# The first loads of a decoder trunk: host layout by partition, another order and other queues

## The chip, the cores and the metric

The kernel runs on one core of a Trainium2 chip. The metric is the device time in microseconds of one execution. Before, three runs took 1038.72, 1039.44 and 1039.55 us, so the median is 1039.44.

## The reference

A trunk of four layers works on 512 tokens of width 1024 in float32: latent attention (MLA), an MLP, gated linear attention (GLA), an MLP. Each is preceded by a root-mean-square norm and added to the residual x. Only the start of the first layer bears on this change:

```python
def rms_norm(x, gain):
    xf = x.astype(jnp.float32)
    y = xf * lax.rsqrt(jnp.mean(xf * xf, axis=-1, keepdims=True) + EPS)
    return (y * gain.astype(jnp.float32)).astype(x.dtype)

def mla_mixer(xn, positions, w_in, q_norm, w_uq, kv_norm, w_ukv, w_o):
    h = xn @ w_in
    c_q = h[..., :Q_LORA]
    c_kv = h[..., Q_LORA:Q_LORA + KV_LORA]
    k_rope = h[..., Q_LORA + KV_LORA:]
    q = (rms_norm(c_q, q_norm) @ w_uq).reshape(B, S, MLA_HEADS, QK_NOPE + QK_ROPE)
    kv = (rms_norm(c_kv, kv_norm) @ w_ukv).reshape(B, S, MLA_HEADS, QK_NOPE + V_HEAD)
```

`w_in` has 1024 rows and 704 columns: 384 for the query, 256 for key and value, 64 for the rotary key. Other weights that the text speaks of: an MLP's up weights have 4096 columns, the GLA's input weights 3088.

## The kernel before

x is kept transposed: `xT` has eight chunks of 128 features (partitions) by 512 tokens. The first projection is therefore a sum over eight chunks k. Products are made in three parts: every operand is split into an upper part (rounded to float32r, written by ScalarE with a Copy) and a lower part (the rest, written by VectorE), and TensorE adds upper x upper, lower x upper and upper x lower. `split` (L122) makes the two parts of weights, `scaled` (L272) the two parts of an x chunk times its norm weight; the token's own norm factor is applied later, which is why the matmuls can start before any sum of squares is known.

The opening is written at the end of `trunk_kernel`. The raw weights of key and value, `raw0` (`wraw_ckv`), come in five pieces (`load_part`, L1683: chunks 0, 1, 2 to 3, 4 to 5, 6 to 7), x in eight (`load_x`, L186), the norm weights with positions in one small load (`gains`, L1689). ScalarE issues x chunks 0 and 1 on its own queue, SP all else. Meanwhile TensorE works on nine matmuls on a tile of ones (L1701). Then for each piece the weights are split (L1704) and the x chunks of that piece scaled (L1707); `tc.keep_in_program_order` holds these ScalarE instructions in the written order. Everything else is placed by a scheduler that orders each engine's instructions by its own estimates, so an edit can move instructions that it does not name.

`mla` (L401) then multiplies. L436 is the projection to key and value, six matmuls for each chunk into two banks, 48 in all. L132 to L134 (`mm3`) are the query's three column blocks: two from `raw` of L444, in two halves of four chunks, and the last from `col_chunk` at L459, loaded at L154. That last load takes the buffer of `wraw_ckv`, so it waits until the last of its splits has read it. `latent` (L410) reads a finished bank twice on ScalarE (L411, L413) and on VectorE (L414, L416). `nrm.square` (L455) forms the squares of x on ScalarE (L265) and sums them on VectorE (L266). The rotary columns are loaded at L467. The means of the three norms are matmuls: L482 of x, L484 of key and value, L486 of the query.

Loads from SP and ScalarE share eight semaphores in turn, so each load waits until the one eight before it has landed.

The rows of `w_in` are 2,816 bytes long. A piece of the key and value weights is thus read in runs of 1 KB, the last query columns in runs of 512 B, the rotary ones in 256 B. An x chunk is 128 runs of 2 KB that lie end to end.

Of the kernel before, what the change touches and what calls it, by code (L numbers as in the profile page):

```python
# [18 lines left out]
P = 128  # L19
# [3 lines left out]
ND = D // P  # L23
# [5 lines left out]
ROPE = 64  # L29
# [21 lines left out]
def trunk_kernel(ctx: ExitStack, tc: tile.TileContext, t_in: dict, out: bass.AP):  # L51
# [70 lines left out]
    def split(src, hi, lo, hi_eng=ACT, lo_eng=DVE, order=lambda i: i):  # L122
        if hi_eng is ACT:
            order(ACT.activation(hi, src, AF.Copy))  # L124
        else:
            hi_eng.tensor_copy(hi, src)
        lo_eng.tensor_tensor(lo, src, f(hi), ALU.subtract)  # L127
# [35 lines left out]

    def piece(raw, a, n, order=lambda i: i, at=(W_AT, W_AT)):
        hi = room_for("wh", a, n, at[0])
        lo = room_for("wl", a, n, at[1])
        split(raw, hi, lo, order=order)
        return hi, lo
# [14 lines left out]
    xT = [xall[:, j] for j in range(ND)]  # L183
    x_in = t_in["x"].rearrange("(j p) t -> p j t", p=P)

    def load_x(q, j):  # L186
        q.dma_start(xall[:, j], x_in[:, j])

# [212 lines left out]
    def mla(layer, nrm, first, pools):  # L401
        w_in = t_in["mla_w_in"][layer]
        w_uq = t_in["mla_w_uq"][layer].rearrange("(k p) (h c) -> p k h c", p=P, h=MH)
# [38 lines left out]
        for h in range(2):  # L442
            ks = slice(h * KH, (h + 1) * KH)
            SP.dma_start(raw[:, ks], w_in[:, :256].rearrange("(k p) n -> p k n", p=P)[:, ks])  # L444
            wq.append(piece(raw[:, ks], KH, 256))
# [12 lines left out]

        raw = col_chunk(w_in, 256, P)  # L459
        w = piece(raw, ND, P)  # L460
# [5 lines left out]

        raw = col_chunk(w_in, QL + KL, ROPE)  # L467
        wr = room_for("wh", ND, 2 * ROPE).rearrange("p k (a b) -> p k a b", a=2)
# [1211 lines left out]
    raw0 = sb.tile([P, ND, 256], F32, tag="wraw", bufs=2, name="wraw_ckv")  # L1680
    src0 = t_in["mla_w_in"][0][:, QL : QL + KL].rearrange("(k p) n -> p k n", p=P)

    def load_part(k0, k1):  # L1683
        SP.dma_start(raw0[:, k0:k1], src0[:, k0:k1])

    load_x(ACT, 0)
    load_part(0, 1)
    load_x(ACT, 1)
    SP.dma_start(gains, t_in["gains"])  # L1689
    load_part(1, 2)  # L1690
    load_part(2, 4)
    load_x(SP, 2)
    load_x(SP, 3)
    for k in (4, 6):
        load_part(k, k + 2)
        load_x(SP, k)
        load_x(SP, k + 1)
    exp_set()
# [4 lines left out]
    for k0, k1 in ((0, 1), (1, 2), (2, 4), (4, 6), (6, 8)):  # L1703
        w = piece(raw0[:, k0:k1], k1 - k0, KL, tc.keep_in_program_order)  # L1704
        w0 += [(w, i) for i in range(k1 - k0)]
        for j in range(k0, k1):
            nrm.scaled(j, xT[j], tc.keep_in_program_order)  # L1707
# [41 lines left out]
_INS = [  # L1749
    "mla_w_in", "mla_w_uq", "mla_w_ukv", "mla_w_o", "gla_w_in", "gla_w_gk_up", "gla_w_o",  # L1750
    "mlp_w_up", "mlp_w_down",
# [21 lines left out]


def layout(inputs):
    arrs = {n: np.ascontiguousarray(inputs[n]) for n in _INS}
    arrs["x"] = np.ascontiguousarray(np.asarray(inputs["x"])[0].T)
    gains = np.concatenate([np.asarray(inputs[n]).reshape(-1, P) for n in GAINS]).T
    positions = np.ascontiguousarray(np.asarray(inputs["positions"]).reshape(NT, P).T)
    inv_freq = np.array([[float.fromhex(v) for v in _INV_FREQ]] * P, dtype=np.float32)  # L1780
    arrs["gains"] = np.ascontiguousarray(np.concatenate([gains, positions.view(np.float32), inv_freq], axis=1))
    arrs["fin_row"] = np.ascontiguousarray(np.asarray(inputs["final_norm"]).reshape(1, D))
    return arrs
# [11 lines left out]
```

## Time and profile before

| what | before |
|---|---|
| median of three runs | 1039.44 us |
| the profiled execution, its own time | 1039.75 us |
| its span | 1038.0 us |
| granted TensorE clock | 0.999 |
| TensorE matmuls busy | 1028.6 us, 99% |
| VectorE busy | 879.2 us, 85% |
| ScalarE busy | 694.5 us, 67% |
| first matmul of the projection (L436) | 5.55 us after the span's start |
| first matmul of the query projection (L132) | 17.63 us |

Times in the profile count from the start of the span. PE is TensorE (PEld its weight loads), DVE VectorE, ACT ScalarE, POOL GpSimd; SPq and ACTq are the queues on which SP and ScalarE issue DMAs. A row of the view in order of time gives the start, the busy time, the engine and line, the tile written and the tile read, and how often; in brackets stand the idle time ahead and what ended it. A DMA row's last number is the time from issue to landing.

### The profile page before, as it was taken

What the parts mean: (1) busy time and instruction counts of PE and PEld (TensorE: products, weight loads), DVE (VectorE), ACT (ScalarE), POOL (GpSimd) and SP (SyncE); (2) the same over time, 40 slices, a digit from 0 to 9 for tenths busy, and PEclk for the clock granted to TensorE, in tenths of its full rate; (3) what the DMA queues carried; (4) which work ended last, traced back from release to release, by engine and by line L of the source; (5) the groups of instructions that cost most, each with busy time, mean ns of one, the idle gap of its engine ahead of it and who ended that gap; (6) DMA issues with size and microseconds to landing.
All of it is one profiled execution on the core that took longest, in us unless ns stands there. A gap on an engine that the chain in (4) does not pass through costs nothing.

```text
span 1038.0 us, 16859 instructions
## 1 busy us (share of the span) xinstructions
PE 1028.6 (99%) x6522; PEld 922.3 (89%) x6522; DVE 879.2 (85%) x1343; ACT 694.5 (67%) x1130; POOL 111.9 (11%) x128
## 2 busy tenths in 40 slices
PE   9999999999999999999999999999999999999997
PEld 7788888899999999998888888888989989989986
DVE  7889976999989989989686399469799999898994
ACT  7667754676776776786445566565677687677784
POOL 7400000411111111100000000000001101111000
PEclk9999999999999999999999999999999999999999
DMA  7501214788788778623212222164678878778422
GB/s 230 128 21 42 72 51 140 206 192 210 187 198 208 179 194 202 159 82 122 91 42 86 89 70 72 51 162 148 143 200 191 192 204 200 189 197 187 121 82 82
DMA packets 120001, 145.85 MB, mean 141 GB/s; under 512 B 9488, under 2 KB 86288, under 8 KB 119920
## 3 DMA queue, kind: packets, MB, share of 16 engines
q1 hardware_dynamic: 95424, 113.57, 34.4%
q0 software_dynamic: 22400, 29.36, 18.2%
q10 hardware_dynamic: 2096, 1.84, 0.6%
q8 instruction: 51, 0.84, 0.3%
q14 instruction: 30, 0.25, 0.1%
HBM read 142.39 MB, written 2.10 MB: 139 GB/s over the span
## 4 chain that ended last, share of the span: by engine, by line
PE 92%; DVE 4%; ACT 2%; DMA 1%; issue 1%; SPq 0%; ACTq 0%; DVEq 0%
PE ps L988 25%; PE ps L1008 13%; PE ps L1001 13%; PE ps L132 10%; PE ps L133 10%; PE ps L134 10%; PE ps L1180 2%; PE ps L149 1%; PE ps L1434 1%; PE ps L1214 1%; PE ps L1561 1%; DVE wl L127 1%; PE ps L436 1%; DMA xT<-in_x_dram 1%; ACT wh L124 1%
## 5 line engine op out<-in xcount | busy, mean ns | idle before, releaser
L124 ACT ACTIVATE wh<-wraw 128x1024 fp32r<-128x1024 f32 x139 | 146.1, 1056 | 114.2 <-PE ps L133 37.6
L127 DVE TENSOR_TENSOR wl<-wraw,wh 128x1024 fp32r<-128x1024 f32 x139 | 169.5, 1221 | 36.7 <-ACT wh L124 35.9
L988 PE MATMUL ps<-T,wh 128*128 128x256 f32 x896 | 154.6, 275 | 0.1
L127 DVE TENSOR_TENSOR wl<-comb,wh 128x1024 fp32r<-128x1024 f32 x112 | 136.6, 1221 | 14.4 <-ACT wh L124 14.4
L124 ACT ACTIVATE wh<-comb 128x1024 fp32r<-128x1024 f32 x112 | 118.6, 1059 | 43.3 <-issue 30.0
L988 PEld LDWEIGHTS ps<-T,wh 128*128 128x128 f32 x896 | 134.9, 188 | 0.4 <-ACT tmp L1018 0.3
L988 PE MATMUL ps<-T,wl 128*128 128x256 f32 x448 | 123.3, 275 | 0.0
L1008 PE MATMUL ps<-wh,set 128*128 128x512 f32 x392 | 122.1, 390 | 0.0
L988 PE MATMUL ps<-set,wh 128*128 128x256 f32 x672 | 116.9, 276 | 0.0
L132 PE MATMUL ps<-set,wh 128*128 128x512 f32 x280 | 109.6, 391 | 0.0
L133 PE MATMUL ps<-set,wh 128*128 128x512 f32 x280 | 109.5, 391 | 0.0
L134 PE MATMUL ps<-set,wl 128*128 128x512 f32 x280 | 109.2, 390 | 0.0
L1001 PE MATMUL ps<-hidden_parts,wh 128*128 128x256 f32 x784 | 105.8, 275 | 0.0
L988 PEld LDWEIGHTS ps<-set,wh 128*128 128x128 f32 x672 | 101.8, 188 | 0.5
L1001 PEld LDWEIGHTS ps<-hidden_parts,wh 128*128 128x128 f32 x784 | 96.7, 188 | 0.0
L988 PE MATMUL ps<-set,wl 128*128 128x256 f32 x336 | 92.5, 275 | 0.0
L1008 PEld LDWEIGHTS ps<-wh,set 128*128 128x128 f32 x392 | 73.6, 188 | 15.2
L988 PEld LDWEIGHTS ps<-T,wl 128*128 128x128 f32 x448 | 84.1, 188 | 0.0
L1008 PE MATMUL ps<-wl,set 128*128 128x512 f32 x196 | 76.3, 389 | 0.0
L988 PEld LDWEIGHTS ps<-set,wl 128*128 128x128 f32 x336 | 63.1, 188 | 0.0
L134 PEld LDWEIGHTS ps<-set,wl 128*128 128x128 f32 x280 | 52.6, 188 | 11.0
L133 PEld LDWEIGHTS ps<-set,wh 128*128 128x128 f32 x280 | 52.6, 188 | 10.9 <-DVE set L765 0.2
(406 smaller groups left out, 2208.7 us busy)
## 6 DMA issues: line engine op xcount, KB each, us to landing
comb<-in_mlp_w_down_dram SPq DMA_DIRECT2D x74, 512.0 KB, 4.4
wraw<-in_mlp_w_up_dram SPq DMA_DIRECT2D x18, 1024.0 KB, 5.6
wraw<-in_mlp_w_up_dram SPq DMA_DIRECT2D x28, 512.0 KB, 5.6
comb<-in_mlp_w_down_dram POOLq DMA_DIRECT2D x28, 512.0 KB, 7.0
wraw<-in_gla_w_in_dram SPq DMA_DIRECT2D x12, 1024.0 KB, 5.2
comb<-in_mlp_w_up_dram SPq DMA_DIRECT2D x14, 512.0 KB, 4.9
comb<-in_mlp_w_up_dram POOLq DMA_DIRECT2D x14, 512.0 KB, 6.2
wraw<-in_mlp_w_up_dram POOLq DMA_DIRECT2D x14, 512.0 KB, 7.7
```

What stands on the lines that cost most here:

```text
L124: order(ACT.activation(hi, src, AF.Copy))
L127: lo_eng.tensor_tensor(lo, src, f(hi), ALU.subtract)
L132: PE.matmul(psum, wh, xh, start=start, stop=False)
L133: PE.matmul(psum, wh, xl, start=False, stop=False)
L134: PE.matmul(psum, wl, xh, start=False, stop=stop)
L149: PE.transpose(psum, src, ident[: src.shape[0], : src.shape[0]])
L436: PE.matmul(p, w[:, i, j * P : (j + 1) * P], x, start=start, stop=stop)
L988: PE.matmul(o, a_, x_, start=start and j == 0 and k == 0 and n == 0, stop=k == KH - 1 and n == 2, skip_group_check=True)
L1001: PE.matmul(o, w_[:, k, j * P : (j + 1) * P], x_[:, ts], start=opens, stop=k == 1 and n == 2, skip_group_check=True)
L1008: PE.matmul(o, x_, w_, start=start and k == 0 and n == 0, stop=k == 1 and n == 2, skip_group_check=True)
L1180: PE.matmul(p, a, x, start=k == 0 and n == 0, stop=k == 3 and n == 2)
L1214: PE.matmul(o, a, b_, start=False, stop=k == 3 and n == 2, skip_group_check=True)
```

## The change

The host lays x out by partition, so that a partition's eight chunks lie end to end (16 KiB for each partition), and cuts the first projection's weights into four arrays laid out in the same way: `q` (256 columns), `last_q` (128), `kv` (256) and `rope` (64). A partition of a piece of n chunks is then one run: 1 KB for one chunk of `kv`, 2 KB for two, 4 KB for four chunks of `q` or `kv` and for all eight of `last_q`, 2 KB for `rope`; x comes in 2 KB runs, or 4 KB for a pair of chunks.

The loads go out in another order. The norm weights are SP's first load. ScalarE issues x chunks 0, 1 and 2. Key and value weights 4 to 7 come in one load, x chunks 4 and 5 and 6 and 7 in one each. The upper part of weight chunk 0 is written by VectorE and no longer by ScalarE.

```diff
-            hi_eng.tensor_copy(hi, src)
+            order(hi_eng.tensor_copy(hi, src))
...
-    def piece(raw, a, n, order=lambda i: i, at=(W_AT, W_AT)):
+    def piece(raw, a, n, order=lambda i: i, at=(W_AT, W_AT), eng=ACT):
         hi = room_for("wh", a, n, at[0])
         lo = room_for("wl", a, n, at[1])
-        split(raw, hi, lo, order=order)
+        split(raw, hi, lo, eng, order=order)
...
-    x_in = t_in["x"].rearrange("(j p) t -> p j t", p=P)
-
-    def load_x(q, j):
-        q.dma_start(xall[:, j], x_in[:, j])
+    x_in = t_in["x"].rearrange("p (j t) -> p j t", j=ND)
+
+    def load_x(q, j, n=1):
+        q.dma_start(xall[:, j : j + n], x_in[:, j : j + n])
...
-            SP.dma_start(raw[:, ks], w_in[:, :256].rearrange("(k p) n -> p k n", p=P)[:, ks])
+            SP.dma_start(raw[:, ks], in_part("q")[:, ks])
...
-        raw = col_chunk(w_in, 256, P)
+        raw = load(in_part("last_q"), ND, P)
...
-        raw = col_chunk(w_in, QL + KL, ROPE)
+        raw = load(in_part("rope"), ND, ROPE)
...
     load_x(ACT, 0)
+    SP.dma_start(gains, t_in["gains"])
     load_part(0, 1)
     load_x(ACT, 1)
-    SP.dma_start(gains, t_in["gains"])
     load_part(1, 2)
+    load_x(ACT, 2)
     load_part(2, 4)
-    load_x(SP, 2)
     load_x(SP, 3)
-    for k in (4, 6):
-        load_part(k, k + 2)
-        load_x(SP, k)
-        load_x(SP, k + 1)
+    load_part(4, 8)
+    load_x(SP, 4, 2)
+    load_x(SP, 6, 2)
...
-        w = piece(raw0[:, k0:k1], k1 - k0, KL, tc.keep_in_program_order)
+        w = piece(raw0[:, k0:k1], k1 - k0, KL, tc.keep_in_program_order, eng=ACT if k0 else DVE)
...
+def by_partition(a):
+    return np.ascontiguousarray(a.reshape(ND, P, -1).transpose(1, 0, 2).reshape(P, -1))
...
-    arrs["x"] = np.ascontiguousarray(np.asarray(inputs["x"])[0].T)
+    arrs["x"] = by_partition(np.asarray(inputs["x"])[0].T)
+    cuts = {"q": (0, 256), "last_q": (256, QL), "kv": (QL, QL + KL), "rope": (QL + KL, QL + KL + ROPE)}
+    for name, (c0, c1) in cuts.items():
+        arrs["mla_w_" + name] = by_partition(w_in[:, c0:c1])
```

In the changed file lines after L399 stand two further down in `mla` (L414 becomes L416). SP's queue, from its first load to the last of this projection, before:

```order
L1684 DMA wraw_ckv<-in_mla_w_in_dram 128x256
L1689 DMA gains<-in_gains_dram 128x87
L1684 DMA wraw_ckv<-in_mla_w_in_dram 128x256
L1684 DMA wraw_ckv<-in_mla_w_in_dram 128x2x256
L187 DMA xT<-in_x_dram 128x512 x2
L1684 DMA wraw_ckv<-in_mla_w_in_dram 128x2x256
L187 DMA xT<-in_x_dram 128x512 x2
L1684 DMA wraw_ckv<-in_mla_w_in_dram 128x2x256
L187 DMA xT<-in_x_dram 128x512 x2
L444 DMA wraw_294<-in_mla_w_in_dram 128x4x256 x2
L154 DMA wraw_412<-in_mla_w_in_dram 128x8x128
L154 DMA wraw_454<-in_mla_w_in_dram 128x8x64
```

The same queue now:

```order
L1689 DMA gains<-in_gains_dram 128x87
L1686 DMA wraw_ckv<-in_mla_w_kv_dram 128x256 x2
L1686 DMA wraw_ckv<-in_mla_w_kv_dram 128x512
L187 DMA xT<-in_x_dram 128x512
L1686 DMA wraw_ckv<-in_mla_w_kv_dram 128x1024
L187 DMA xT<-in_x_dram 128x1024 x2
L446 DMA wraw_291<-in_mla_w_q_dram 128x1024 x2
L154 DMA wraw_409<-in_mla_w_last_q_dram 128x1024
L154 DMA wraw_451<-in_mla_w_rope_dram 128x512
```

Three loads fewer stand in it, one x chunk has gone to ScalarE's queue, and with the eight semaphores the load of weight chunks 4 to 7 now waits for the norm weights, the two x pairs for x chunk 0 and weight chunk 0, and the two halves of the query weights for x chunk 1 and weight chunk 1.

VectorE from x chunks 4 and 5 to the first sum of squares, before (`wl` is a lower part of weights, `ps_244` and `ps_245` are the banks of key and value):

```order
L277 SCALAR_TENSOR_TENSOR set<-xT,gains,set 128x512 x2
L127 TENSOR_TENSOR wl_163<-wraw_ckv,wh_162 128x512
L1719 CAST ident_i<-ident 128x128
L277 SCALAR_TENSOR_TENSOR set<-xT,gains,set 128x512 x2
L127 TENSOR_TENSOR wl_297<-wraw_294,wh_296 128x1024
L127 TENSOR_TENSOR wl_302<-wraw_294,wh_301 128x1024
L414 SCALAR_TENSOR_TENSOR set_331<-ps_244,gains,set_330 128x512
L127 TENSOR_TENSOR wl_415<-wraw_412,wh_414 128x1024
L414 SCALAR_TENSOR_TENSOR set_337<-ps_245,gains,set_336 128x512
L416 TENSOR_TENSOR set_333<-set_333,tmp_339 128x512
```

The same place now:

```order
L1720 CAST ident_i<-ident 128x128
L277 SCALAR_TENSOR_TENSOR set<-xT,gains,set 128x512 x2
L127 TENSOR_TENSOR wl_160<-wraw_ckv,wh_159 128x512
L277 SCALAR_TENSOR_TENSOR set<-xT,gains,set 128x512 x2
L127 TENSOR_TENSOR wl_294<-wraw_291,wh_293 128x1024
L127 TENSOR_TENSOR wl_299<-wraw_291,wh_298 128x1024
L127 TENSOR_TENSOR wl_412<-wraw_409,wh_411 128x1024
L416 SCALAR_TENSOR_TENSOR set_328<-ps_241,gains,set_327 128x512
L416 SCALAR_TENSOR_TENSOR set_334<-ps_242,gains,set_333 128x512
L418 TENSOR_TENSOR set_330<-set_330,tmp_336 128x512
```

The cast of the identity has moved ahead of x chunks 4 and 5, and the lower part of the last query weights ahead of both reads of the banks of key and value. ScalarE from the first half of the query weights to the first squares, before:

```order
L124 ACTIVATE wh_296<-wraw_294 128x1024
L124 ACTIVATE wh_301<-wraw_294 128x1024
L411 ACTIVATE set_330<-ps_244,gains 128x512
L413 ACTIVATE set_333<-ps_244 128x512
L124 ACTIVATE wh_414<-wraw_412 128x1024
L411 ACTIVATE set_336<-ps_245,gains 128x512
L413 ACTIVATE tmp_339<-ps_245 128x512
```

The same place now:

```order
L124 ACTIVATE wh_293<-wraw_291 128x1024
L124 ACTIVATE wh_298<-wraw_291 128x1024
L124 ACTIVATE wh_411<-wraw_409 128x1024
L413 ACTIVATE set_327<-ps_241,gains 128x512
L415 ACTIVATE set_330<-ps_241 128x512
L413 ACTIVATE set_333<-ps_242,gains 128x512
L415 ACTIVATE tmp_336<-ps_242 128x512
```

The split of the last query weights has moved ahead of the reads of the first bank here too. TensorE's order and GpSimd's are the same as before. Between 26 and 36 us a few more lower and upper parts change places on ScalarE and VectorE (the second value weights, the sums of squares); from there on the order is the same on every engine.

More of the change, by code (lines that the diff above doesn't have):

```diff
@@ L401, in mla, with in_part @@
     def mla(layer, nrm, first, pools):
-        w_in = t_in["mla_w_in"][layer]
+        def in_part(name):
+            return t_in["mla_w_" + name].rearrange("p (k n) -> p k n", k=ND)
         w_uq = t_in["mla_w_uq"][layer].rearrange("(k p) (h c) -> p k h c", p=P, h=MH)
@@ L1680, in trunk_kernel @@
     raw0 = sb.tile([P, ND, 256], F32, tag="wraw", bufs=2, name="wraw_ckv")
-    src0 = t_in["mla_w_in"][0][:, QL : QL + KL].rearrange("(k p) n -> p k n", p=P)
+    src0 = t_in["mla_w_kv"].rearrange("p (k n) -> p k n", k=ND)
     def load_part(k0, k1):
@@ L1749 @@
 _INS = [
-    "mla_w_in", "mla_w_uq", "mla_w_ukv", "mla_w_o", "gla_w_in", "gla_w_gk_up", "gla_w_o",
+    "mla_w_uq", "mla_w_ukv", "mla_w_o", "gla_w_in", "gla_w_gk_up", "gla_w_o",
     "mlp_w_up", "mlp_w_down",
@@ L1772, in build @@
         trunk_kernel(tc, args, o)
+def by_partition(a):
+    return np.ascontiguousarray(a.reshape(ND, P, -1).transpose(1, 0, 2).reshape(P, -1))
 def layout(inputs):
     arrs = {n: np.ascontiguousarray(inputs[n]) for n in _INS}
-    arrs["x"] = np.ascontiguousarray(np.asarray(inputs["x"])[0].T)
+    arrs["x"] = by_partition(np.asarray(inputs["x"])[0].T)
+    w_in = np.asarray(inputs["mla_w_in"])[0]
+    cuts = {"q": (0, 256), "last_q": (256, QL), "kv": (QL, QL + KL), "rope": (QL + KL, QL + KL + ROPE)}
+    for name, (c0, c1) in cuts.items():
+        arrs["mla_w_" + name] = by_partition(w_in[:, c0:c1])
     gains = np.concatenate([np.asarray(inputs[n]).reshape(-1, P) for n in GAINS]).T
```

## The prediction

> **What bounds the kernel now.** I read the page first, then busy time by stretches of the opening, then the chain of waits, the instructions in order of time, and the DMA issues. On the page:
>
> ```profile
> PE 1028.6 (99%) x6522; PEld 922.3 (89%) x6522; DVE 879.2 (85%) x1343; ACT 694.5 (67%) x1130; POOL 111.9 (11%) x128
> ```
>
> TensorE idles 9.4 us of a span of 1038.0 us. By stretches (PE, PEld, DVE, ACT, POOL, granted clock, DMA share, GB/s):
>
> ```profile
> 0.00:5.55 5.55, 4.21 (x19) 3.92 (x19) 1.43 (x17) 2.48 (x4) 1.59 (x10) 1.00 0.63 188
> 5.55:10.00 4.45, 3.86 (x15) 2.91 (x16) 3.55 (x5) 3.04 (x6) 4.05 (x9) 1.00 0.96 307
> 10.00:17.40 7.40, 7.40 (x33) 5.93 (x32) 7.13 (x11) 6.50 (x9) 6.91 (x10) 1.00 0.98 314
> 26.32:37.60 11.28, 11.28 (x52) 9.30 (x51) 11.28 (x14) 6.38 (x10) 10.31 (x15) 1.00 0.62 143
> ```
>
> Only the first 10 us have idle TensorE time that this change can reach. From 10 us on VectorE is nearly as full as TensorE, and it is entirely full from 26.32 to 37.60. So whatever makes TensorE earlier must make VectorE as much earlier. Then what sets the opening, first by the chain of waits (in all fences rows are picked, and those between them left out):
>
> ```profile
> 0.80 0.39 SPq L1684
> 1.25 0.41 SPq L1689
> 2.66 5.78 DMA xT<-in_x_dram
> 8.46 0.73 ACT set L276
> 9.23 8.56 PE ps L436 x36
> 17.79 0.23 PE ps L132
> ```
>
> The instructions in order of time (start, busy, engine, and in brackets the idle time ahead):
>
> ```profile
> 0.80 0.89 ACTq L187 DMA_DIRECT2D xT<-in_x_dram  x2
> 1.18 4.21 PE L1701 MATMUL ps<-ones 128*128 128x128 f32 x18 [1.18 <-DVE ones L195]
> 4.77 0.72 ACT L276 ACTIVATE set<-xT,gains 128x512 fp32r<-128x512 f32 x1 [0.39 <-DMA gains<-in_gains_dram]
> 7.71 0.63 ACT L124 ACTIVATE wh<-wraw_ckv 128x512 fp32r<-128x512 f32 x1 [1.29 <-DMA wraw_ckv<-in_mla_w_in_dram]
> 8.37 0.69 DVE L127 TENSOR_TENSOR wl<-wraw_ckv,wh 128x512 fp32r<-128x512 f32 x1 [0.76 <-ACT wh L124]
> 9.21 1.68 DVE L277 SCALAR_TENSOR_TENSOR set<-xT,gains,set 128x512 fp32r<-128x512 f32 x2
> 11.77 1.64 DVE L277 SCALAR_TENSOR_TENSOR set<-xT,gains,set 128x512 fp32r<-128x512 f32 x2
> 13.34 0.77 DVE L127 TENSOR_TENSOR wl<-wraw_ckv,wh 128x512 fp32r<-128x512 f32 x1
> 14.13 5.03 SPq L154 DMA_DIRECT2D wraw<-in_mla_w_in_dram  x2
> ```
>
> Chunk 2 of x, the third, lands at 8.44 (2.66 + 5.78), ScalarE scales it, and at 9.23 TensorE starts 36 matmuls that run through with one short gap. Weight chunks 2 and 3 had landed at 7.71. The moment at which VectorE starts the low part of x chunk 2 (9.21) I call T: from there both engines run on without a gap that matters, so **the change is worth what it takes off T**, if nothing later takes it back. The other end of the argument is at 39 us:
>
> ```profile
> 35.03 1.31 DVE L127 TENSOR_TENSOR wl<-wraw_qr,wh 128x1024 fp32r<-128x1024 f32 x1
> 38.30 0.69 DVE L127 TENSOR_TENSOR set<-set,set 128x512 fp32r<-128x512 f32 x1 [0.70 <-ACT set L124]
> 39.04 0.47 PE L486 MATMUL ps<-set,mean_q 128*96 128x512 f32 x1
> ```
>
> VectorE ends the query's sum of squares at 38.99, and TensorE's second L486 matmul takes it at 39.04. There is no slack: the kernel gains the smaller of what TensorE and what VectorE gained. The order of instructions after the opening is unchanged on all five engines, apart from lower and upper parts on VectorE and ScalarE that change places before 36 us, so a shift at 39 us goes through to the end.
>
> **The change part by part.** *First matmul.* The norm weights go out at about 0.80 instead of 1.25, and the first weight chunk at 1.25 instead of 0.80. The first scaling waited for the norm weights until 4.77, so it starts up to 0.45 us sooner. That is worth nearly nothing: the warm-up matmuls hold TensorE until 5.39 (1.18 + 4.21). The rest of TensorE's way from 5.39 gives a ceiling: 48 matmuls of L436 at the 0.23 us of the L132 row end at 16.4, against 17.79 now, so no version of this change gains more than 1.4 us.
>
> *The copy that moves to VectorE.* The upper part of weight chunk 0 becomes a cast of 128x256 on VectorE. Before shows no such cast; ScalarE does it in 0.42, and a 128x128 cast on VectorE takes 0.32:
>
> ```profile
> 14.03 0.32 DVE L1719 CAST ident_i<-ident 128x128 int32<-128x128 f32 x1
> 3.96 0.42 ACT L124 ACTIVATE wh<-wraw_ckv 128x256 fp32r<-128x256 f32 x1 [0.96 <-DMA wraw_ckv<-in_mla_w_in_dram]
> 5.53 0.79 DVE L277 SCALAR_TENSOR_TENSOR set<-xT,gains,set 128x512 fp32r<-128x512 f32 x1 [0.69 <-ACT set L276]
> 6.24 0.68 DVE L127 TENSOR_TENSOR wl<-wraw_ckv,wh 128x256 fp32r<-128x256 f32 x1
> 6.84 0.77 DVE L277 SCALAR_TENSOR_TENSOR set<-xT,gains,set 128x512 fp32r<-128x512 f32 x1
> ```
>
> Between 0.2 and 0.6 us, then; I take 0.35. With chunk 0 landed at 4.4 (3.96 + 0.45), cast 0.35, low part 0.42, x0 0.79, low part 0.68, x1 0.77, VectorE is through chunk 1 at 7.4 (7.66 at 0.6), where it is at 7.61 now and then waits 0.76 us for ScalarE. The cast lies under that wait. Without it, it would cost its 0.35.
>
> *T.* Now ScalarE splits weight chunks 2 and 3 while x chunk 2 is in flight. In the new order x chunk 2 goes out as the third load of ScalarE's queue (about 1.7 instead of 2.66), beside weight chunks 2 and 3 on SP's. T is then the weights' landing plus 0.63 (split) plus 0.73 (scaling), 1.38 with the gaps. When do they land? The bytes moved in each of the first 40 us, the packets of the 14th of them, the landings of x, and the issue and landing of its chunk 4:
>
> ```profile
> GB/s 0 16 199 384 327 251 269 262 312 387 395 382 362 348 279 135 306 149 0 27 198 48 36 268 334 297 128 0 38 238 255 225 38 199 337 230 14 0 0 0
> DMA packets 352, 0.35 MB, mean 348 GB/s; under 512 B 12, under 2 KB 352, under 8 KB 352
> DMA to landing us min/median/max: 3.3/5.9/6.4
> 4.58 0.94 SPq L187 DMA_DIRECT2D xT<-in_x_dram  x2
> xT<-in_x_dram SPq DMA_DIRECT2D x1, 256.0 KB, 6.0
> ```
>
> Norm weights, weight chunks 0 to 3 and x chunks 0 to 2 are 1.355 MB. By 5 us 0.926 MB had moved. At 0.39 MB per us, the rate of 9 to 12 us, the rest takes 1.1 us more (6.1); x chunk 0 (0.262 MB, reached at 3.1) landed at 4.1 (0.80 + 3.3), 1.0 after its bytes by this sum. That is the early end: 7.1, T = 8.5. At the rate of 5 to 8 us the sum is reached at 6.7, and x chunk 2, which stood at the same sum, landed 1.8 later: 8.44, T = 9.8. Between them stands today's row for these weights, 7.71 (T = 9.1). I take 7.3, on the early side of it, since these weights are now 2 KB runs and not 1 KB ones: the microsecond from 13 us, which moved no packet of 2 KB, made 348 GB/s, the mixed ones from 9 us up to 395. T = 8.7, **0.5 us gained**.
>
> The Trainium skill, "DMA: Bandwidth & Descriptors", section Specifications, says that transfers of 512 B and more reach line rate, and that HBM gives a core about 358 GB/s. By that longer runs would bring nothing; with 358 in place of 390 the early end is 7.2 instead of 7.1. The trace disagrees with the limit: 387, 395 and 382 GB/s in three microseconds on end.
>
> *Pairs of x and four weight chunks in one load.* Chunks 4 to 7 of the weights come as one load, x in pairs. That is three loads fewer, and each goes out by about 6 us, since the load that it has to wait for, eight before it, lands by then; but chunk 4 of x now lands with chunk 5. VectorE wants x chunk 4 at T + 2.8 (9.21 to 11.77 now, and 0.23 for a cast of the identity that the scheduler puts ahead of it), so the pair must be down by T + 2.05, 10.75. The bytes up to it are 2.666 MB: early 5 + 1.74 / 0.39 + 1.0 = 10.5; late, at today's sums (10.7) plus the 1.3 by which x chunk 4 was behind its own (2.142 MB at 9.3, landed at 4.58 + 6.0), 12.0. I take the early end, as for T: it just fits, at no cost.
>
> *The last query weights.* ScalarE now splits them ahead of both results of the first projection, VectorE likewise. Behind that split stand, on ScalarE, the four reads of the first projection's banks and the squares of x, and VectorE's sums wait for these; TensorE waits for none of it before L486. Their load waits until VectorE has read weight chunks 6 and 7 (13.34 + 0.77; issued at 14.13). In the new order that is 14.13 + 0.23 less the gain g on T.
>
> ```profile
> wraw<-in_mla_w_in_dram SPq DMA_DIRECT2D x1, 512.0 KB, 4.3
> comb<-in_fin_row_dram SPq DMA_DIRECT2D x1, 512.0 KB, 3.5
> 19.76 1.23 DVE L127 TENSOR_TENSOR wl<-wraw,wh 128x1024 fp32r<-128x1024 f32 x1 [0.20 <-ACT wh L124]
> 21.57 0.80 DVE L416 TENSOR_TENSOR set<-set,tmp 128x512 f32<-128x512 f32 x1
> ```
>
> It lands 4.3 later now, in 512 B runs. After, its runs are 4 KB; the one load of 4 KB rows in the trace, also 512 KB, takes 3.5. With 3.5: landed at 17.86 - g, low part from 1.10 later (split), then 1.14, 0.67, 0.67 to the place that stands at 21.57: 21.44 - g. VectorE keeps g, and 0.13 more. With 4.3 it keeps g - 0.67: this is the step that can swallow the gain. I take 3.5.
>
> Sum: 1039.75 (the profiled execution: its span and 1.75 around it) less 0.5 is 1039.25. The median of the runs is 0.31 below the profiled one, so I forecast **1038.9**.
>
> **The rivals.** *Swallowed.* The last query weights land 4.3 after issue: 0.5 - 0.67, within 0.2 of nothing, 1039.4 to 1039.6. For it: ScalarE and VectorE then stand idle before that split. Against: 4 KB runs. *Later pairs, slower.* Today's slow 5 to 8 us stay, and the pair with x chunk 4 lands at 12.0: VectorE starts its low part at 12.7 where it does at 11.77 now; less the 0.23 that is moved, 0.7 late, and 1.4 if the last query weights take 4.3 too: 1040.1 to 1040.8. It decides from a landing after 11.3. For it: nothing explains 251 to 269 GB/s at 5 to 8 us. *To the ceiling.* Loads land by 6.7 as if no packet were late: 1.0 to 1.4 gained, 1038.0 to 1038.4. *Row pitch.* Partitions now lie 16 KiB (x) and 8 KiB (weights) apart in HBM, powers of two. The nearest rows:
>
> ```profile
> wraw<-in_mlp_w_up_dram SPq DMA_DIRECT2D x2, 1024.0 KB, 5.5
> wraw<-in_gla_w_in_dram SPq DMA_DIRECT2D x1, 1024.0 KB, 5.1
> ```
>
> The first has rows 16 KiB apart, the second 12,352 B: 0.4 us per MB, 1.1 on 2.67 MB: the pair at 11.6, 0.3 after the landing that decides, 1039.7. At half the rate it would land at 14.9: 1043.1. The skill's same page, section Latency and other measured facts, has a slowdown for large power-of-two pitches, from 512 KiB on; no run here has such a pitch, and ours lie far below it.
>
> **How the numbers follow.** Forecast (0.2 to 1.0 gained) 50%, swallowed 20%, later pairs 17%, ceiling 10%, pitch 3%. Runs of one kernel spread over 0.8 us. From the ceiling with half of that spread (1037.7) to the later pairs (1040.4) leaves out under 2 in 10. A measurement can tell 0.2%, 2.1 us: the ceiling of 1.4 is below it, so faster is left 2%, slower 4% (half rate, or a wait that I do not see), and the rest is the same.
>
> **What would show it.** The first L436 matmul at 5.4 to 5.5; T between 8.5 and 9.1; the x pair 4 and 5 down by 10.75 with no idle VectorE before it; the last query weights 3.5 us after their issue; the second L486 matmul at about 38.5. I am wrong if T stays at 9.2, if VectorE waits for x chunk 4, or if L486 moves by other than the whole time does.

## The result, and the profile after

| | before | after |
|---|---|---|
| median of 13 runs each, us | 1039.31 (1038.72 to 1040.07) | 1041.53 (1040.55 to 1042.35) |
| ratio to before, 95% interval | | 1.0021 [1.0014, 1.0029] |
| profiled execution: time, span, granted clock | 1039.75, 1038.0, 0.999 | 1041.53, 1039.8, 0.999 |

The change makes the kernel 2.2 us (0.2%) slower; forecast was 1038.9 (1037.7 to 1040.4). The spreads of the two sets of runs do not overlap. TensorE's busy time is the same 1028.6 us, so the loss is idle time. The page of after, and its busy time by stretches (same columns as in the prediction):

```profile
PE 1028.6 (99%) x6522; PEld 921.4 (89%) x6522; DVE 879.0 (85%) x1344; ACT 693.5 (67%) x1129; POOL 111.7 (11%) x128
```

```profile
0.00:5.74 5.74, 3.67 (x19) 3.50 (x19) 1.43 (x17) 2.00 (x2) 2.50 (x12) 1.00 0.60 160
5.74:10.93 5.19, 3.67 (x13) 2.14 (x14) 3.04 (x5) 2.51 (x5) 4.70 (x12) 1.00 0.97 350
10.93:18.90 7.97, 7.97 (x35) 6.23 (x35) 7.97 (x13) 6.51 (x10) 7.49 (x11) 1.00 0.65 254
```

From the first projection matmul (5.74) to T (10.93) TensorE now idles 1.52 us (5.19 less 3.67); from T on it is full again. The chain of waits says what it waited for:

```profile
2.19 7.24 DMA wraw_ckv<-in_mla_w_kv_dram
...
9.45 0.63 ACT wh L124
10.08 0.62 ACT set L276
...
10.74 8.69 PE ps L438 x36
```

Before, x chunk 2 stood at this place (2.66 + 5.78); now it is weight chunks 2 and 3, 7.24 us after their issue. In order of time (here as below rows are picked):

```profile
5.26 0.33 DVE L126 CAST wh<-wraw_ckv 128x256 fp32r<-128x256 f32 x1 [3.24 <-DMA wraw_ckv<-in_mla_w_kv_dram]
...
5.74 0.70 PE L438 MATMUL ps<-set,wh 128*128 128x512 f32 x2 [0.90 <-DVE wh L126]
...
7.04 0.42 ACT L124 ACTIVATE wh<-wraw_ckv 128x256 fp32r<-128x256 f32 x1 [2.15 <-DMA wraw_ckv<-in_mla_w_kv_dram]
...
9.45 0.63 ACT L124 ACTIVATE wh<-wraw_ckv 128x512 fp32r<-128x512 f32 x1 [1.38 <-DMA wraw_ckv<-in_mla_w_kv_dram]
...
10.93 1.47 DVE L277 SCALAR_TENSOR_TENSOR set<-xT,gains,set 128x512 fp32r<-128x512 f32 x2
...
12.69 1.34 ACT L276 ACTIVATE set<-xT,gains 128x512 fp32r<-128x512 f32 x2 [0.67 <-DMA xT<-in_x_dram]
...
13.73 1.49 DVE L277 SCALAR_TENSOR_TENSOR set<-xT,gains,set 128x512 fp32r<-128x512 f32 x2
...
23.34 0.69 DVE L418 TENSOR_TENSOR set<-set,tmp 128x512 f32<-128x512 f32 x1
...
40.59 0.46 PE L488 MATMUL ps<-set,mean_q 128*96 128x512 f32 x1
```

Every weight load is late: the instructions that wait for them start at 5.26 (chunk 0), 7.04 (chunk 1) and 9.45 (chunks 2 and 3). Before, these splits started at 3.96, 5.40 (without waiting) and 7.71. T is 10.93 against 9.21 (+1.72), the second matmul of the query's mean is at 40.59 against 39.04 (+1.55), the span 1.8 longer. The bytes moved in each microsecond, and the landing of the last query weights:

```profile
GB/s 0 16 214 293 209 252 282 311 371 399 414 422 418 397 193 49 29 164 332 0 0 184 84 108 306 329 287 29 8 0 41 270 242 212 22 54 270 341 122 0
...
wraw<-in_mla_w_last_q_dram SPq DMA_DIRECT2D x1, 512.0 KB, 3.4
```

From 3 to 8 us the longer runs move 209 to 311 GB/s, from 9 to 14 us 397 to 422. The rate is lost where T is decided. But it is not the rate alone: the 1.355 MB of the loads up to weight chunks 2 and 3 had moved at 7.3 us by this row, and these weights were there only at 9.45, so bytes of later loads moved meanwhile.

### The profile page after: what moved, and what is told of

It is laid out like the page before. It is cut to its first block, busy times and chain, and to the rows that moved or that the text cites. A ratio compares the mean times of both kernels' runs of the same rounds, so it can differ in the third digit from the quotient of the medians.

```text
span 1039.8 us, 16854 instructions
## 1 busy us (share of the span) xinstructions
PE 1028.6 (99%) x6522; PEld 921.4 (89%) x6522; DVE 879.0 (85%) x1344; ACT 693.5 (67%) x1129; POOL 111.7 (11%) x128
## 4 chain that ended last, share of the span: by engine, by line
PE 92%; DVE 4%; ACT 2%; DMA 1%; issue 1%; SPq 0%; ACTq 0%; DVEq 0%
PE ps L990 25%; PE ps L1010 13%; PE ps L1003 13%; PE ps L132 10%; PE ps L133 10%; PE ps L134 10%; PE ps L1182 2%; PE ps L149 1%; PE ps L1436 1%; PE ps L1216 1%; PE ps L1563 1%; DVE wl L127 1%; PE ps L438 1%; DMA wraw_ckv<-in_mla_w_kv_dram 1%; ACT wh L124 1%
```

## The experiments

Times are medians of 11 runs each, against the kernel before on the same chip (21 or 33 runs, medians 1039.19 to 1039.43). "By partition" is the new layout, "old" that of before, "by chunk" means that the rows of a chunk lie end to end. "Split 2-3" is ScalarE's start on weight chunks 2 and 3, "mean" the second matmul of the query's mean; both and T are from the one profiled execution of each kernel.

| run | layout of x; kv weights | order | less before, us | ratio, 95% interval | split 2-3 | T | mean |
|---|---|---|---|---|---|---|---|
| (before) | old; old | old | | | 7.71 | 9.21 | 39.04 |
| (after) | by partition | new | +2.22 | 1.0021 [1.0014, 1.0029] | 9.45 | 10.93 | 40.59 |
| layout_only | by partition | old | +0.69 | 1.0006 [0.9997, 1.0015] | 7.90 | 9.33 | 39.10 |
| order_only | old; old | new | +0.56 | 1.0005 [0.9996, 1.0014] | 6.98 | 8.34 | 38.95 |
| x2_on_sp | by partition | new, x2 on SP | +1.08 | 1.0013 [1.0004, 1.0022] | 7.67 | 9.27 | 40.43 |
| no_pairs | by partition | new, six loads | +1.14 | 1.0011 [1.0002, 1.0020] | 8.55 | 9.85 | 39.63 |
| x2_sp_no_pairs | by partition | new, both | +1.41 | 1.0013 [1.0004, 1.0021] | 7.50 | 8.93 | 39.27 |
| x_old_layout | old; by partition | new | +1.01 | 1.0009 [1.0001, 1.0018] | 8.09 | 9.50 | 39.51 |
| w_old_layout | by partition; old | new | +1.09 | 1.0011 [1.0002, 1.0019] | 7.87 | 9.37 | 39.54 |
| w_chunks | old; by chunk | new | +0.02 | 1.0001 [0.9992, 1.0010] | 7.24 | 8.52 | 39.38 |
| q_new_only | old; old | new | +0.37 | 1.0004 [0.9995, 1.0013] | 6.79 | 8.07 | 38.65 |
| q_new_no_pairs | old; old | new, six loads | -0.17 | 0.9998 [0.9989, 1.0006] | 7.11 | 8.41 | 38.39 |
| w_chunks_no_pairs | old; by chunk | new, six loads | -0.26 | 0.9998 [0.9989, 1.0007] | 6.83 | 8.11 | 38.02 |
| padded | by partition + 256 B | new | +0.69 | 1.0004 [0.9995, 1.0014] | 8.31 | 9.68 | 39.70 |
| padded_no_pairs | by partition + 256 B | new, six loads | +0.22 | 1.0005 [0.9996, 1.0014] | 8.24 | 9.73 | 39.53 |
| padded_old_order | by partition + 256 B | old | +0.06 | 1.0000 [0.9991, 1.0009] | 6.86 | 8.30 | 38.21 |

One profiled execution can sit anywhere in the 0.7 to 1.8 us over which a kernel's runs spread (that of w_chunks, 1040.28, was its slowest; that of padded_old_order, 1038.75, its second fastest). The medians decide; the profiles tell the place. After, order_only, q_new_only, x_old_layout, w_old_layout, w_chunks and padded run the same instructions in the same order on ScalarE and VectorE from start to end, so no difference among these seven comes from the scheduler; the same holds within the pairs before and layout_only, layout_only and padded_old_order, no_pairs and padded_no_pairs, q_new_no_pairs and w_chunks_no_pairs.

**Halves of the change.** layout_only takes before's loads, order and cast; order_only the old layout of x and of all four weight arrays.

Against after, layout_only has the block of loads of before, and

```diff
-        w = piece(raw0[:, k0:k1], k1 - k0, KL, tc.keep_in_program_order, eng=ACT if k0 else DVE)
+        w = piece(raw0[:, k0:k1], k1 - k0, KL, tc.keep_in_program_order)
```

and order_only, with the host's arrays and the views of the query and rotary weights likewise,

```diff
-    x_in = t_in["x"].rearrange("p (j t) -> p j t", j=ND)
+    x_in = t_in["x"].rearrange("(j p) t -> p j t", p=P)
...
-    src0 = t_in["mla_w_kv"].rearrange("p (k n) -> p k n", k=ND)
+    src0 = t_in["mla_w_in"][0][:, QL : QL + KL].rearrange("(k p) n -> p k n", p=P)
```

> The host layout by partition with the loads, queues and copies of before. Layout theory (the wide pitch of the partitions in HBM makes the first loads slow): +1.5 to +2.2 us on the kernel before, weight chunks 2 and 3 landed after 9 us. Queue theory (x chunk 2 on ScalarE's queue holds up the small weight loads): within 0.4 us of before, chunks 2 and 3 landed by 7.8, the last query weights 3.4 us after their issue.

> The new order, queues, pairs and the cast on VectorE with the old layout of x and weights. Layout theory: -0.5 to +0.3 us on before, weight chunk 1 landed by 5.6. Queue theory: +1.5 to +2.5 us, weight chunk 1 landed near 7, chunks 2 and 3 after 9.

Alone they cost 0.69 and 0.56, together 2.22: they make each other worse. Neither theory had this: by the first the layout alone was to cost 1.5 or more, by the second the order alone. In order_only the early loads are what I had forecast. Its bytes and the rows at T:

```profile
GB/s 0 9 139 394 395 366 378 344 348 399 384 369 347 326 86 213 266 1 26 203 38 84 260 319 301 97 8 0 47 237 238 235 29 3 187 329 251 17 0 0
```

```profile
8.34 1.64 DVE L277 SCALAR_TENSOR_TENSOR set<-xT,gains,set 128x512 fp32r<-128x512 f32 x2
...
10.67 1.34 ACT L276 ACTIVATE set<-xT,gains 128x512 fp32r<-128x512 f32 x2 [0.72 <-DMA xT<-in_x_dram]
...
11.43 1.45 DVE L277 SCALAR_TENSOR_TENSOR set<-xT,gains,set 128x512 fp32r<-128x512 f32 x2 [0.25 <-ACT set L276]
...
17.64 1.06 ACT L124 ACTIVATE wh<-wraw 128x1024 fp32r<-128x1024 f32 x1 [1.47 <-DMA wraw<-in_mla_w_in_dram]
...
18.73 1.23 DVE L127 TENSOR_TENSOR wl<-wraw,wh 128x1024 fp32r<-128x1024 f32 x1 [0.96 <-ACT wh L124]
```

344 to 395 GB/s from 3 to 8 us, and T at 8.34. But the mean is only 0.09 earlier than before: the pair of x costs 0.3 (x chunk 4 starts at T + 3.09, not T + 2.8), and the last query weights, here in 512-byte runs and split ahead of both banks, let VectorE wait 0.96.

**One edit of the order undone**, layout by partition: the first piece of this diff is x2_on_sp, the second no_pairs, both together x2_sp_no_pairs.

```diff
-    load_x(ACT, 2)
     load_part(2, 4)
+    load_x(SP, 2)
...
-    load_part(4, 8)
-    load_x(SP, 4, 2)
-    load_x(SP, 6, 2)
+    for k in (4, 6):
+        load_part(k, k + 2)
+        load_x(SP, k)
+        load_x(SP, k + 1)
```

> The changed kernel, but x chunk 2 on SP's queue behind weight chunks 2 and 3. Queue theory: weight chunk 1 lands by 5.8 and not 7.0, chunks 2 and 3 by 8.0 and not 9.45, -1.2 to -1.8 us on the changed kernel (+0.4 to +1.0 on before). Layout theory: no more than 0.5 us better than the changed kernel.

> The changed kernel, but weight chunks 4 to 7 and x chunks 4 to 7 in the six loads of before. Pair theory (the large loads land late): -0.8 us or more on the changed kernel. Queue and layout theory: within 0.4 us of the changed kernel (+1.8 to +2.6 on before), since the first late step, chunks 2 and 3, is untouched.

> The changed kernel, both layouts new, with both later edits undone together: x chunk 2 on the SP queue and the six loads. What is left of the reorder is the gains ahead of the weights and the cast on VectorE. If the two edits' costs add (1.0 and 1.0 us as undone one by one): 1039.5 to 1039.7. If both undo the same stall (too many bytes asked for behind the first weights), less than the sum comes back: 1040.0 to 1040.5, near the layout alone (1040.12).

Each gives back about 1.1 us, both together 0.8, less than was expected if both undo the same stall. So they are no separate terms. My reading is that either one lets fewer bytes compete with the weights that land first; this is not shown. no_pairs gives back what its pair theory asked for, but through T (9.85), not behind it. In x2_on_sp T falls to 9.27 and in x2_sp_no_pairs to 8.93, but in both the scheduler now puts a read of the first bank (L413) ahead of the split of the last query weights, and the mean comes 31.2 and 30.3 after T instead of 29.7. So these two change more than their edit says, and their times weigh less here.

**One tensor's layout undone**, new order. x_old_layout and w_old_layout have the x and the weight half of order_only's edit; q_new_only has x and the kv weights old, the query and rotary weights by partition; w_chunks is x_old_layout and, with the host's array likewise,

```diff
-    src0 = t_in["mla_w_kv"].rearrange("p (k n) -> p k n", k=ND)
+    src0 = t_in["mla_w_kv"].rearrange("(k p) n -> p k n", p=P)
```

> The changed kernel with x alone back in its old layout (rows of a chunk 2 KiB long and 2 KiB apart; the weights stay laid out by partition, rows 8 KiB apart). X-pitch theory (x's rows 16 KiB apart are what stalls the first loads, for every load that shares the engines): weights chunk 1 lands by 6.0 us, chunks 2 and 3 by 7.2, VectorE starts the low part of x chunk 2 at 8.4, time 1039.5 to 1040.0. Weight-pitch theory (the weights' rows 8 KiB apart are the cause): chunk 1 at 6.8 to 7.1, chunks 2 and 3 at 9.0 to 9.5, low part of chunk 2 at 10.5 to 10.9, time 1041.2 to 1041.6. If each layout does half: 1040.5 to 1040.9.

> The changed kernel with the first projection's weights alone back in their old layout (x stays by partition, rows 16 KiB apart). X-pitch theory: chunks 2 and 3 still land at 9.0 or later, low part of x chunk 2 at 10.5 or later, and the last query weights come by 512-byte runs, 4.0 to 4.3 us after issue: 1041.3 to 1042.0. Weight-pitch theory: weights chunk 1 by 6.0, chunks 2 and 3 by 7.2, low part at 8.4, and the last query weights then set the end as in the run with both layouts old: 1039.7 to 1040.2.

> The changed kernel with x in its old layout and the key/value weights cut out but contiguous by chunk (rows 1 KiB long and 1 KiB apart); the query and rotary weights stay by partition. Pitch theory: no early load has rows 8 or 16 KiB apart, so chunks 2 and 3 land by 7.2, the low part of x chunk 2 starts at 8.4 or before, the last query weights land 3.4 us after issue, and the time is 1038.8 to 1039.5, under the run with both layouts old (1039.99). Queue theory (small loads queued behind large ones, whatever their rows): chunks 2 and 3 after 8.5, 1040.5 to 1041.5.

> The changed kernel with x and the key/value weights in their old layout; only the query and rotary weights lie by partition. It differs from the run with all layouts old (1039.99) in the last query weights' runs, 4 KiB for 512 bytes. Swallowing theory (with the early gain in hand, the last query weights set the end): they land 3.4 instead of 4.0 us after issue, ScalarE's wait of 1.47 us ahead of their split falls under 1.0, and the time is 1039.2 to 1039.6. If the layout change of any tensor costs by itself (code, descriptors): 1040.0 or more.

With either tensor by partition the loss is halved (+1.01, +1.09). That was not expected so: 1040.20 lies below the range for halves (1040.5 to 1040.9), and 1040.28 just over the one for the weights' pitch alone (1039.7 to 1040.2). With neither tensor by partition the loss is gone (+0.02 by chunk, +0.37 old; both in their ranges). w_chunks has the changed kernel's order, queues, pairs, cast and query weights: **from after it differs only in where the rows of x and the kv weights lie in HBM** (and so in the runs of weights 2 to 7 and of the x pairs, which are shorter), and that is worth 2.2 us. The queue theory falls with it. Its rows at T and its bytes:

```profile
7.24 0.64 ACT L124 ACTIVATE wh<-wraw_ckv 128x512 fp32r<-128x512 f32 x1 [0.21 <-DMA wraw_ckv<-in_mla_w_kv_dram]
...
8.52 1.64 DVE L277 SCALAR_TENSOR_TENSOR set<-xT,gains,set 128x512 fp32r<-128x512 f32 x2
```

```profile
GB/s 0 14 149 393 376 380 365 346 331 391 412 408 410 246 20 86 311 127 0 92 178 8 180 332 315 216 6 8 0 117 288 218 164 0 48 326 269 143 0 0
```

From 3 to 8 us it moves 346 to 393 GB/s, where after moves 209 to 311. The longer runs as the cause are still open here; the padding below keeps them.

**The pairs, once the rows are right.**

> The run with only the query and rotary weights by partition (1039.56), with weights 4 to 7 and x 4 to 7 in the six loads of before. Pair theory (the gain of 1.1 us at the low part of x chunk 2 is eaten by ScalarE's waits of 0.7 us each for weights 4 to 7 and the pair of x): both waits shrink to under 0.3, the low part of x chunk 4 starts at 11.0 or earlier (11.48 with pairs), the second matmul of the mean about 0.5 earlier, and the time is 1038.7 to 1039.2. If the issue of six loads for three delays the query weights: 1039.5 or more.

> The run with x old and key/value weights contiguous by chunk (1039.21), with the six loads of before for weights 4 to 7 and x 4 to 7. Pair theory: waits of 0.78 and 0.73 us for weights 4 to 7 and the pair of x shrink to under 0.3, time 1038.4 to 1038.9. Else 1039.2 or more.

The six loads in place of three take 0.54 and 0.28 off, as the pair theory has it in sign; neither difference is clear of the noise (1039.12 is in its range, 1039.03 between its two). With pairs (q_new_only) and without:

```profile
8.07 1.64 DVE L277 SCALAR_TENSOR_TENSOR set<-xT,gains,set 128x512 fp32r<-128x512 f32 x2
...
10.72 1.34 ACT L276 ACTIVATE set<-xT,gains 128x512 fp32r<-128x512 f32 x2 [0.72 <-DMA xT<-in_x_dram]
...
11.48 1.50 DVE L277 SCALAR_TENSOR_TENSOR set<-xT,gains,set 128x512 fp32r<-128x512 f32 x2 [0.46 <-ACT set L276]
```

```profile
8.41 1.64 DVE L277 SCALAR_TENSOR_TENSOR set<-xT,gains,set 128x512 fp32r<-128x512 f32 x2
...
9.95 1.42 ACT L276 ACTIVATE set<-xT,gains 128x512 fp32r<-128x512 f32 x2 [0.46 <-DMA xT<-in_x_dram]
...
10.81 1.47 DVE L277 SCALAR_TENSOR_TENSOR set<-xT,gains,set 128x512 fp32r<-128x512 f32 x2
```

x chunk 4 is taken at 11.48 (T + 3.41) with pairs, at 10.81 (T + 2.40) without, and the mean follows T by 30.6 with and 30.0 without. w_chunks_no_pairs, 0.26 under before, is the fastest kernel tried, and not told apart from before.

**The pitch by itself.** 256 bytes behind each row: kv rows 8,448 B apart for 8,192, x 16,640 for 16,384. Loads and runs stay.

```diff
-    arrs["x"] = by_partition(np.asarray(inputs["x"])[0].T)
+    arrs["x"] = np.pad(by_partition(np.asarray(inputs["x"])[0].T), ((0, 0), (0, 64)))
-        arrs["mla_w_" + name] = by_partition(w_in[:, c0:c1])
+        arrs["mla_w_" + name] = np.pad(by_partition(w_in[:, c0:c1]), ((0, 0), (0, 64 if name == "kv" else 0)))
```

> The changed kernel with 256 bytes of padding behind each row: key/value weights 8448 bytes apart for 8192, x 16640 for 16384; loads, order and runs unchanged. Power-of-two theory (it is the pitch of 8 and 16 KiB that stalls packets, as many rows then meet in the same place of the memory): weights chunk 1 lands by 6.0 us, chunks 2 and 3 by 7.3, low part of x chunk 2 at 8.1 to 8.6, time 1039.0 to 1039.7, as with weights by chunk (1039.21). Spread theory (rows far apart are slow at any wide pitch): chunk 1 at 7.0, low part at 10 to 11, time 1041.0 to 1042.0.

> The changed kernel with padded rows and the six loads of before for weights 4 to 7 and x 4 to 7. Two terms, pitch and pairs: if they are separate, the pairs' cost (0.3 to 0.4 as seen with the query weights alone and with weights by chunk) comes off the padded run's 1039.98: 1039.0 to 1039.6, level with before. If padding cures only part of the late loads because the rows still lie far apart, 1039.7 to 1040.2, like no_pairs without padding (1040.57) less a part.

> Before's loads, order and cast, with the layout by partition and the padding. Power-of-two theory: against the unpadded layout in the old order (1040.12, 0.7 above before) it wins 0.5 or more: 1039.2 to 1039.6. If in the old order something else than the pitch costs the 0.7 (longer runs in the same queues): 1039.9 to 1040.3.

Padding takes off 1.5 in the new order (2.22 to 0.69), 0.9 without pairs (1.14 to 0.22; 0.7 by the means, since three of its eleven runs lie above 1040), 0.6 in the old order (0.69 to 0.06). Three pairs of kernels that differ in nothing else agree in sign. The intervals within a pair touch or overlap, but the slowest run of padded (1040.49) is faster than the fastest of after (1040.55). In padded the rows at T and the bytes are these:

```profile
6.87 0.42 ACT L124 ACTIVATE wh<-wraw_ckv 128x256 fp32r<-128x256 f32 x1 [2.06 <-DMA wraw_ckv<-in_mla_w_kv_dram]
...
8.31 0.63 ACT L124 ACTIVATE wh<-wraw_ckv 128x512 fp32r<-128x512 f32 x1 [0.42 <-DMA wraw_ckv<-in_mla_w_kv_dram]
...
9.68 1.47 DVE L277 SCALAR_TENSOR_TENSOR set<-xT,gains,set 128x512 fp32r<-128x512 f32 x2
```

```profile
GB/s 0 9 223 378 286 295 342 334 416 410 426 418 430 234 41 53 250 221 0 33 225 20 97 281 298 275 94 11 0 37 274 241 214 21 24 252 322 185 4 0
```

From 3 to 8 us padded moves 286 to 378 GB/s, between after and w_chunks. I had expected a whole cure for the new order, and padding is not one: padded takes 1039.98 where I expected 1039.0 to 1039.7, and weight chunk 1 is still split at 6.87 in padded and 7.30 in padded_no_pairs.

The packets in the same traces (the pieces in which a load is moved) say what a late load is made of. Of those that start between 2 and 9 us most take the same time in every layout (46 ns for 1 KB, 84 for 2 KB, 159 for 4 KB); a few take over three times as long. There are 44 in after and 45 in its repeat below, 4 to 10 in the five kernels with the new order and no early row by partition, and 23 and 33 in padded and padded_no_pairs: padding removes a part of them, old or contiguous rows nearly all. In the old order the old layout has many too (47 in before, 24 in its repeat).

**The loads alone.** Two kernels, one execution each, do nothing but the ten opening loads of x and the key and value weights in the changed order, six times; a VectorE addition that reads what a pass brought ends each. From probe_wide to probe_near:

```diff
-    for src in (wide, wide, near, near, padded, padded):
+    for src in (near, near, wide, wide, padded, padded):
         one_pass(*src)
```

> Leaves out the whole computation: only the opening's ten loads of x and the key/value weights, in the changed kernel's order and queues, six passes one after the other (each waits until VectorE has read what the last one brought): both tensors by partition (rows 8 and 16 KiB apart) twice, contiguous by chunk twice, by partition with 256 bytes of padding twice. Pitch theory: 3 MiB by partition takes longer than contiguous in both its passes, the padded ones like the contiguous. First-touch theory (the first access to a stretch of memory stalls): each layout's first pass is slower than its second by 1 us or more. Opening theory (only the first 9 us of a program stall): the first pass alone is slow, all later ones within 0.5 us of one another, about 3.1 MB at 400 GB/s, 8 us, and 2 us of latency.

> Leaves out the whole computation, as the other probe, with the contiguous layout first: contiguous twice, by partition twice, padded twice. Pitch theory: passes 3 and 4 are the slow ones, by the same amount as passes 1 and 2 of the other probe. First-touch theory: passes 1, 3 and 5 each slower than 2, 4 and 6, pass 3 most. Opening theory: pass 1 alone is slow, and as slow as by partition.

The end of each pass and, in brackets, how long VectorE waited for it, first of probe_wide, then of probe_near ("in_x" is by partition, "near" by chunk, "pad" padded):

```profile
13.73 0.17 DVE L76 TENSOR_TENSOR junk<-xT,wraw_ckv 128x8 f32<-128x8 f32 x1 [13.73 <-DMA xT<-in_x_dram]
26.63 0.17 DVE L76 TENSOR_TENSOR junk<-xT,wraw_ckv 128x8 f32<-128x8 f32 x1 [12.73 <-DMA xT<-in_x_dram]
39.72 0.17 DVE L76 TENSOR_TENSOR junk<-xT,wraw_ckv 128x8 f32<-128x8 f32 x1 [12.91 <-DMA xT<-in_x_near_dram]
51.75 0.17 DVE L76 TENSOR_TENSOR junk<-xT,wraw_ckv 128x8 f32<-128x8 f32 x1 [11.86 <-DMA xT<-in_x_near_dram]
63.39 0.18 DVE L76 TENSOR_TENSOR junk<-xT,wraw_ckv 128x8 f32<-128x8 f32 x1 [11.47 <-DMA xT<-in_x_pad_dram]
75.49 0.17 DVE L76 TENSOR_TENSOR junk<-xT,wraw_ckv 128x8 f32<-128x8 f32 x1 [11.92 <-DMA xT<-in_x_pad_dram]
```

```profile
12.49 0.17 DVE L76 TENSOR_TENSOR junk<-xT,wraw_ckv 128x8 f32<-128x8 f32 x1 [12.49 <-DMA xT<-in_x_near_dram]
24.86 0.17 DVE L76 TENSOR_TENSOR junk<-xT,wraw_ckv 128x8 f32<-128x8 f32 x1 [12.20 <-DMA xT<-in_x_near_dram]
37.99 0.17 DVE L76 TENSOR_TENSOR junk<-xT,wraw_ckv 128x8 f32<-128x8 f32 x1 [12.95 <-DMA xT<-in_x_dram]
51.06 0.17 DVE L76 TENSOR_TENSOR junk<-xT,wraw_ckv 128x8 f32<-128x8 f32 x1 [12.89 <-DMA xT<-in_x_dram]
61.59 0.17 DVE L76 TENSOR_TENSOR junk<-xT,wraw_ckv 128x8 f32<-128x8 f32 x1 [10.36 <-DMA xT<-in_x_pad_dram]
72.94 0.17 DVE L76 TENSOR_TENSOR junk<-xT,wraw_ckv 128x8 f32<-128x8 f32 x1 [11.17 <-DMA xT<-in_x_pad_dram]
```

Leaving out the first pass of each (it holds the start of the program), by partition takes 12.73, 12.95 and 12.89, by chunk 12.91, 11.86 and 12.20, padded 11.47, 11.92, 10.36 and 11.17. The two first passes differ in the same way, 13.73 by partition and 12.49 by chunk. By partition is slow whether it comes first or later and on its second pass too: neither the first touch nor the first microseconds of a program make it. The padded passes are the fastest, although their rows lie as far apart; I had expected them to be like those by chunk, of which one (12.91) is as slow as by partition. (They come last in both; a drift with place is not seen, since by chunk is no slower ahead of by partition than behind it.) The landing of the 256 KB load of weight chunks 2 and 3, median of two passes, in probe_near:

```profile
wraw_ckv<-in_kv_near_dram SPq DMA_DIRECT2D x2, 256.0 KB, 5.4
...
wraw_ckv<-in_mla_w_kv_dram SPq DMA_DIRECT2D x2, 256.0 KB, 7.2
...
wraw_ckv<-in_kv_pad_dram SPq DMA_DIRECT2D x2, 256.0 KB, 4.7
```

7.2 is the changed kernel's 7.24 of the chain of waits, found again with all engines idle. In probe_wide it is 7.3, 6.5 by chunk, 5.3 padded.

**Repeats.** One more profiled execution of each kernel.

> The changed kernel once more, one look: if the late weights are the layout's and order's doing, chunk 1 lands at 6.8 to 7.2 us and the low part of x chunk 2 starts at 10 to 11 again; if they were the profiled execution's own bad luck, chunk 1 lands under 6.5.

> The kernel before once more, one look: how far its opening varies. The profiled execution of before took 1039.75 against a median of 1039.3 over all runs, so VectorE's start of the low part of x chunk 2 should come some 0.4 us before the 9.21 of that profile, at 8.8, if the opening is what varies.

After repeats itself: chunk 1 split at 6.97, chunks 2 and 3 at 9.59, T 10.86, mean 40.57, 1041.26. Before does not:

```profile
7.19 0.64 ACT L124 ACTIVATE wh<-wraw_ckv 128x512 fp32r<-128x512 f32 x1 [0.73 <-DMA wraw_ckv<-in_mla_w_in_dram]
...
8.62 1.45 DVE L277 SCALAR_TENSOR_TENSOR set<-xT,gains,set 128x512 fp32r<-128x512 f32 x2
...
38.50 0.47 PE L486 MATMUL ps<-set,mean_q 128*96 128x512 f32 x1
```

```profile
GB/s 0 20 174 383 365 346 334 345 376 339 390 373 359 345 170 288 157 0 0 126 143 30 196 337 308 183 11 5 173 276 219 123 218 326 223 10 0 0 0 0
```

T is 8.62 for 9.21 (8.8 expected), and the slow stretch of before's first profile (251 to 269 GB/s from 5 to 8 us) is not there: 346, 334 and 345. From the two repeats T is 2.24 later after the change and the mean 2.07, close to the 2.2 of the medians.

## Why the prediction was wrong

- **The step that failed is the landing of weight chunks 2 and 3** in the part on T: taken at 7.3, with bounds 7.1 and 8.44; measured 9.45 and 9.59. I chose the early side of today's 7.71 because 2 KB runs should move faster than 1 KB ones, and priced the run's length alone. w_chunks and padded show that where a run lies costs more than its length brings. Both terms of the landing were too small: the sum of bytes was reached at 7.3 (6.1 to 6.7 in the prediction), and the weights were there 2.2 us after it (1.0 to 1.8). The 0.5 us gained on T became 1.7 lost.
- **The rival of the row pitch had the cause, at 3%.** Its price, 0.4 us per MB from the rows of two large loads, was spread over 2.67 MB and charged to the pair of x chunks (1039.7, or 1043.1 at half the rate). The delay falls on the small first loads, ahead of T: about 2 us on 1.355 MB. Of the 2.2 us padding takes off 1.5; the rest goes with the layout too (w_chunks), by a way that is not shown. The Trainium skill, "DMA: Bandwidth & Descriptors", section Latency and other measured facts, gives the slowdown for pitches from 512 KiB on. I took 16 KiB as far below that; the padded runs show the effect at 8 and 16 KiB. The Trainium skill's remark there that a few KiB of padding restore the rate where 192 B do not was measured on larger pitches; here 256 B take off 0.6 to 1.5 us.
- **The gain itself was half an accident of one execution.** "Nothing explains 251 to 269 GB/s at 5 to 8 us" was the warning. I left these microseconds in the bounds, but took T = 9.21 as the kernel's. Its repeat has 8.62, so T = 8.7 was no gain. I took 0.31 off the total for the profiled execution's excess, and not off the gain. With old or contiguous rows the new order comes out at +0.02 to +0.56 with pairs and at -0.17 and -0.26 without: no gain that the runs can tell from nothing.
- *Everything after T goes through one to one*: right for the loss. The mean follows T by 29.8 before, 29.7 after, 29.9 and 29.7 in the repeats, and from the mean to the end of the span it is 998.6 to 999.4 us in all eighteen profiles of a whole kernel. The loss is T's. It would not have been right for the gain: where T came at 8.07 to 8.52 with pairs (q_new_only, order_only, w_chunks), the mean followed by 30.6 to 30.9.
- *The cast*: right, 0.33 for 0.35, under VectorE's wait. *First matmul*: 5.74 for 5.4 to 5.5, since weight chunk 0 was there at 5.26 and not 4.4. It costs nothing beside what comes after.
- *Pairs*: the need (T + 2.05) was right, the landing not: 12.69 for 10.5. In after this costs nothing behind T, as T is late itself (10.93 + 2.80 = 13.73). Where T is early it bites: in order_only and q_new_only the pair lands at 10.67 and 10.72, 0.3 and 0.6 behind T + 2.05, and VectorE starts x chunk 4 that much late. My early end (10.5) was missed by only 0.2, and with T that early it was not early enough.
- *Last query weights*: right, 3.4 after issue for 3.5. In 512-byte runs (order_only) it was 3.9, and VectorE then waited 0.96 ahead of their low part (0.43 in after). How much of the gain that swallowed is not separated from the pair's part.

That both halves together cost more than their sum is seen in the medians, and why is not shown. By 6 us the changed kernel has issued 1.6 MB behind its first eight loads, the kernel before 1.0 MB; no_pairs, which is back at 1.0, gives 1.1 us back, but so does x2_on_sp, which stays at 1.6. Nor is it shown what the rows share, or that a power of two is what matters: one padding was tried, 256 B on both tensors at once, and it also changes where each array begins.

## What to carry to other kernels

A layout in which every partition's row starts a power of two behind the last one can be slower to load than short runs end to end, here at 8 and 16 KiB; try padded rows, or lay each load's rows end to end, and price the layout on the first loads, where nothing covers it. Before a gain is read off a stall of 0.5 us, look at a second profile: a stretch with unexplained low GB/s may belong to one execution. When a first stage gets faster, ask for each later load whether it now comes by when it is wanted: large joint loads land as one.

## What the runs showed of the hardware

- Loads of the same 3 MiB with the same queues, first passes left out, take 10.4 to 11.9 us with rows 8,448 and 16,640 B apart, 12.7 to 13.0 with 8,192 and 16,384 B. Contiguous chunks lie between (11.9 to 12.9), which I had not expected and cannot explain.
- One core moved 397 to 422 GB/s over five microseconds on end (after, from 9 us), where before had reached 395.
- The 512 KB load of the last query weights landed in 3.4 to 3.6 us with 4 KB runs in twelve profiles with the new order (3.9 and 4.2 in two with the old), and in 3.9 to 4.3 with 512-byte runs in four.
- The loss sits in few packets: 44 and 45 of those that start between 2 and 9 us took over three times the usual in after and its repeat, 7 in w_chunks, with the same loads in the same order.
